# A hybrid decoder block: retention's projection as two Strassen passes, and retention itself beside the output projection

## The chip, the cores and the metric

The kernel runs on one core of a Trainium2 chip. The metric is device time in microseconds (us) of one execution of the whole program. The engines are TensorE (PE in the profile, with its weight loads shown apart as PEld), VectorE (DVE), ScalarE (ACT), GpSimd (POOL) and SyncE (SP, which issues most DMAs). PSUM has eight banks of 128x512 float32; they are what TensorE writes to.

## The reference

One decoder layer over 1024 tokens of width 1024, in float32:

```
h    = RMSNorm(x)
proj = h @ w_in                        # 1024 x 3584: rq rk rv rg (512 each), dq dk dv (512 each)
ret  = retention(rq, rk, rv)           # 8 heads of 64; rotary on q and k; chunks of 128 tokens
ret  = RMSNorm_per_head(ret) * silu(rg)
dif  = differential attention(dq, dk, dv)   # 4 heads, two causal softmax maps per head
x    = x + concat([ret, RMSNorm_per_head(dif)]) @ w_out
x    = x + (silu(h2 @ w_gate) * (h2 @ w_up)) @ w_down     # h2 = RMSNorm(x), d_ff = 2816
```

Retention of one head and one chunk of 128 tokens: `inner = (q k^T) * decay`, `o = inner v + (q * q_dec) state`, `state = state * chunk_dec + (k * k_dec)^T v`. The state makes the chunks of one head sequential.

## The kernel before

Every large product is done in three matmuls of the fast float32r type: an operand is split into a high half (a cast to float32r, on ACT) and a low half (the difference, on DVE), and `mm3` adds hi·hi, hi·lo and lo·hi. Small products (turns of tiles by the identity, retention's own matmuls, attention's values) are plain float32.

The program is a sequence of stages. In each stage the function `run(ops, main)` (line 509) takes eight steps of a main product, one for each 128 rows of the contraction, and puts small pieces of work between the steps. The tables `DIF_PLAN` (line 76) and `RET_PLAN` (line 104) say for each piece how many stages behind the product it runs, and behind which step. The order is pinned: instructions stay on their engine in the order in which they were issued. All pinned instructions pass through one helper (`issue`, line 375), so nearly all rows of the profile have line 376, and one goes by the names of tiles.

- Stages 0 to 31: projection and differential attention of 4 heads x 8 token tiles, `proj(g, t)` with 384 columns. The normed and turned activations stay on the chip as `hT` (tile name `act`). In `d_qz` GpSimd makes the cast `qz`; `rsqrt` is a power on GpSimd. The scores (`d_scores`, bank `big`) read `qz` two steps into the next stage.
- Stages 32 to 63: projection of retention, 4 pairs of heads x 8 token tiles, with 512 columns (q, k, v and gate of two heads): 24 matmuls of 128x512 a stage. Behind it go the pieces of the unit of two heads: `r_rot` (rotary, value scaling, gate), `r_turn`, `r_take` (ACT copies q and k out of PSUM, and q again by halves), `r_inner`, `r_mask`, `r_state`, `r_decay`, `r_out`, `r_sq` and `r_norm`. The inner products and the outputs have banks of their own, two of each (`it`, `o`).
- Three stages `o_proj(t, 0)` with the last pieces of retention, then `mid()`: the other 13 half-row tiles of the output projection, the norm, and the first 14 Strassen products of gate and up. The table `MID_PLAN` (line 121), some 200 rows written out by hand, places the small work there.
- Gate and up, 11 groups of 256 columns, each in seven products (Strassen's scheme over 2x2 blocks), and then down, in seven products of 11 chunks. Their order follows from program order and rings of tiles.

The weights of the projections are loaded one stage ahead (256 KB for each 128 rows) and split by ACT and DVE.

## Time and profile before

| | us |
| --- | --- |
| runs (three) | 1210.06, 1210.2, 1211.38 (median 1210.2) |
| span of the profiled execution | 1208.6 |
| differential stages | 0 to 250.9 |
| retention stages | 250.9 to 475.2 |
| output projection and norm | 475.2 to 587.3 |
| gate and up | 587.3 to 992.2 |
| down | 992.2 to 1208.6 |

The borders are read from the timeline (first and last matmul of the bank concerned). The page gives busy time for each engine, then the span in 40 slices, the DMA queues, the chain of work that ended last, and the costliest groups of instructions. A group's row has its busy time and the mean of one instruction behind the bar, and behind the next bar the idle time of the engine just before these instructions with what ended it. In a timeline a row starts with its start and its length, and the idle time before it stands in brackets. A run of equal instructions shares one row. Starts of TensorE's rows are firmer than their ends: matmuls overlap, so the distance of two starts is the time that one takes.

### The profile page before, as it was taken

The page shows a single profiled execution, that of the slowest core. Times are in us where ns is not written, and L with a number is a line of the kernel's source. Part 1 is how long each engine was busy: PE and PEld are TensorE (multiplying, and loading weights), DVE is VectorE, ACT ScalarE, POOL GpSimd, SP SyncE. Part 2 cuts the span into 40 slices and gives each one's busy share as a digit, 9 for nine tenths or more (in the row PEclk, how much of TensorE's full clock was granted, in tenths as well). Part 3 has the DMA queues.
Part 4 walks back from the last instruction along what each step waited for, and adds up shares of the span by engine and source line. Part 5 has one row for each costly group of instructions (what it writes and reads, how often), then busy time and mean ns, then how long its engine had stood idle before and what let it go on. Part 6 is the DMA issues. An engine that isn't in the chain of part 4 may idle for free.

```text
span 1208.6 us, 17360 instructions
## 1 busy us (share of the span) xinstructions
PE 1199.0 (99%) x5968; PEld 1020.0 (84%) x5968; DVE 834.1 (69%) x1501; ACT 537.6 (44%) x1194; POOL 556.6 (46%) x709
## 2 busy tenths in 40 slices
PE   8999999999999999999999999999999999999998
PEld 7898989888888888888888888888888888888887
DVE  6988888854444445545988765766657559698697
ACT  6866666653222233434634344333443434444442
POOL 2655555644444443200066556554566536254053
PEclk9999999999999999999999999999999999999999
DMA  7200011103111110332233323423333178943332
GB/s 209 62 28 27 28 30 35 45 10 97 48 40 36 40 40 27 122 123 79 61 123 118 109 96 114 131 83 92 105 113 127 65 238 287 366 129 96 96 122 79
DMA packets 97239, 117.08 MB, mean 97 GB/s; under 512 B 8960, under 2 KB 60288, under 8 KB 97152
## 3 DMA queue, kind: packets, MB, share of 16 engines
q1 hardware_dynamic: 95824, 115.38, 29.8%
q8 instruction: 47, 0.77, 0.3%
q10 hardware_dynamic: 1328, 0.60, 0.2%
q14 instruction: 40, 0.33, 0.1%
HBM read 87.38 MB, written 28.57 MB: 96 GB/s over the span
## 4 chain that ended last, share of the span: by engine, by line
PE 96%; DVE 2%; ACT 1%; DMA 0%; issue 0%; SPq 0%; ACTq 0%; DVEq 0%
PE pp L376 44%; PE h L376 27%; PE m L376 19%; PE big L376 3%; PE o L376 2%; PE it L376 1%; DVE act L376 0%; DMA more<-in_w_in_dram 0%; DVE q L376 0%; DVE acc L376 0%; ACT kh L376 0%; DVE wlo L376 0%; DVE kl L376 0%; DVE sum L376 0%; DVE kh L376 0%
## 5 line engine op out<-in xcount | busy, mean ns | idle before, releaser
L376 PE MATMUL pp<-whi,act 128*128 128x384 f32 (+1 forms) x896 | 286.4, 372 | 0.3 <-ACT whi L376 0.3
L376 POOL TENSOR_TENSOR sum<-rawp 128x512 f32<-128x512 f32 x100 | 142.1, 1423 | 174.2 <-DVE wlo L376 172.6
L376 ACT CAST whi<-sum 128x512 fp32r<-128x512 f32 x165 | 102.6, 622 | 202.2 <-POOL sum L376 66.0
L376 DVE TENSOR_TENSOR wlo<-sum,whi 128x512 fp32r<-128x512 f32 x165 | 165.7, 1005 | 35.2 <-ACT whi L376 35.0
L376 PE MATMUL h<-act,whi 128*128 128x512 f32 x608 | 187.2, 389 | 0.0
L376 PEld LDWEIGHTS pp<-whi,act 128*128 128x128 f32 x896 | 166.6, 188 | 15.1 <-ACT whi L376 0.7
L376 PE MATMUL pp<-wlo,act 128*128 128x384 f32 (+1 forms) x448 | 161.2, 360 | 0.6 <-DVE wlo L376 0.6
L376 POOL TENSOR_TENSOR sum<-wide 128x512 f32<-128x512 f32 x55 | 87.1, 1586 | 127.2 <-DVE wlo L376 100.2
L376 PEld LDWEIGHTS h<-act,whi 128*128 128x128 f32 x608 | 114.0, 188 | 23.6
L376 PE MATMUL pp<-wrh,act 128*128 128x512 f32 x384 | 131.3, 402 | 0.0
L376 PE MATMUL h<-act,wlo 128*128 128x512 f32 x304 | 118.3, 389 | 0.0
L376 DVE TENSOR_TENSOR wlo<-wide,whi 128x512 fp32r<-128x512 f32 x99 | 78.8, 819 | 32.6 <-ACT whi L376 32.6
L376 PE MATMUL pp<-act,whi 128*128 128x512 f32 (+2 forms) x320 | 97.2, 385 | 0.2 <-DVE act L376 0.2
L376 PE MATMUL m<-act,whi 128*128 128x512 f32 (+2 forms) x320 | 97.0, 385 | 0.0
L376 ACT CAST whi<-wide 128x512 fp32r<-128x512 f32 x99 | 59.3, 621 | 83.2 <-PE m L376 43.3
L376 PEld LDWEIGHTS pp<-wlo,act 128*128 128x128 f32 x448 | 84.6, 189 | 7.8 <-DVE wlo L376 1.2
L376 PEld LDWEIGHTS pp<-wrh,act 128*128 128x128 f32 x384 | 72.2, 188 | 14.3
L376 POOL TENSOR_TENSOR fsum<-c 128x512 f32<-128x512 f32 x55 | 79.4, 1454 | 9.6 <-DMA ffd<-fsum 9.6
L376 DVE TENSOR_TENSOR c<-c,h 128x512 f32<-128x512 f32 x86 | 56.8, 681 | 30.4 <-PE h L376 30.4
L376 PE MATMUL pp<-wrl,act 128*128 128x512 f32 x192 | 74.9, 390 | 0.0
L376 DVE TENSOR_TENSOR wlo<-rawp,whi 128x512 fp32r<-128x512 f32 x44 | 47.5, 1079 | 38.9 <-ACT whi L376 38.1
L376 PEld LDWEIGHTS pp<-act,whi 128*128 128x128 f32 x320 | 59.9, 188 | 12.2 <-DVE act L376 0.4
(163 smaller groups left out, 2514.2 us busy)
## 6 DMA issues: line engine op xcount, KB each, us to landing
wide<-ffd SPq DMA_DIRECT2D x77, 256.0 KB, 2.7
ffd<-fsum SPq DMA_DIRECT2D x55, 256.0 KB, 2.0
rawp<-in_w_gate_dram SPq DMA_DIRECT2D x22, 512.0 KB, 3.8
rawp<-in_w_up_dram SPq DMA_DIRECT2D x22, 512.0 KB, 3.8
wide<-in_w_down_dram SPq DMA_DIRECT2D x44, 256.0 KB, 5.4
raw<-in_w_in_dram SPq DMA_DIRECT2D x32, 256.0 KB, 2.8
ffd<-c SPq DMA_DIRECT2D x22, 256.0 KB, 2.0
raw<-in_w_in_dram SPq DMA_DIRECT2D x26, 192.0 KB, 2.5
```

The source lines that it names most:

```text
L376: i = getattr(self.engine, op)(*args, **kw)
```

## The change

Retention's projection is no longer 32 stages of 24 matmuls. Its 1024 x 1024 by 1024 x 2048 product is cut into two passes of 1024 columns (the q, k, v and gate columns of four heads each), and each pass is done by seven products of blocks half as long in every direction, as in Strassen's scheme. A product is four tiles (128 tokens) of four row blocks of `mm3`: 48 matmuls of 128x512. Pass `p=0` computes P1, P2, P4, P6, P7, P5, P3; pass `p=1` P1, P2, P6, P5, P3, P7, P4.

The sums of activation blocks that four of the products need are built in DRAM while the differential stages run: in stages 8 to 30 `s_sum` stores or copies a block (SP) or adds one to it with an accumulating DMA that GpSimd issues, two calls a stage, 40 accumulations in 20 stages. Later `x_sum` loads a sum and splits it. Sums of weight blocks are made per product out of two to four raw pages (`prepare`: GpSimd subtracts, ACT scales, DVE adds and splits). The products are combined by DVE (or ACT, or GpSimd once) into output tiles, which are stored in DRAM (`cd`) and read again by retention.

In the last three stages of the differential part, where the tail of attention still runs, `lead` does the first 72 matmuls of pass 0, and a table `LEAD` makes the weights of P4 there. From there to the first products of gate and up all work is a list of jobs with engine, duration and the keys that it reads and writes. `Plan` simulates the engines with these durations, four rounds, takes on each engine the ready job that is due first, and the jobs are issued, pinned, in the order of their starts. `RET_PLAN`, `MID_PLAN` and their pieces are gone.

Retention is done in units of four heads and 128 tokens (`unit`), 16 instead of 32. Four of them stand beside pass 1, twelve beside the output projection, whose tiles go in the order `PAIRS`. The unit has one bank each for its turn, its inner products, and its output with its state update. The differential part is otherwise as it was, and so are gate, up and down after their first products.

The first place is GpSimd in one differential stage. In the rows, `rs4` is the reciprocal root of q and k's mean squares, `qz` the cast, `mo` and `ro` the output's norm, `rowa` the attention's output. Before:

```order
L376 TENSOR_TENSOR rs4_1934<-ms4_1932,cs_77 128x4
L376 CAST qz1_186<-q_1995 64x128 x2
L376 TENSOR_SCALAR epso_2015<-ls_1975 128x1
L376 TENSOR_SCALAR mo_2023<-so_2021,epso_1902 128x1
L376 TENSOR_TENSOR ro_2025<-mo_2023,cs_77 128x1
L376 TENSOR_SCALAR rowa_94<-ob_2018,ro_2025 128x128
```

The same place in the change:

```order
L136 TENSOR_TENSOR rs4_2077<-ms4_2075,cs_77 128x4
L136 DMA sumd_196<-act_88 128x512 x2
L136 CAST qz0_185<-q_2144 64x128 x2
L136 TENSOR_SCALAR epso_2164<-ls_2120 128x1
L136 TENSOR_SCALAR mo_2172<-so_2170,epso_2045 128x1
L136 TENSOR_TENSOR ro_2174<-mo_2172,cs_77 128x1
L136 TENSOR_SCALAR rowa_95<-ob_2167,ro_2174 128x128
```

Two accumulating DMAs now stand between the root and the cast on GpSimd's queue.

The second place is TensorE in retention. Before, in a retention stage (`it` the inner products, `o` the output, `m` a state update or a turn, `pp` the projection):

```order
L376 MATMUL it_5280<-qbd1_3632,qkT_5253 128x256
L376 MATMUL m_5282<-vh_5194,qkr_5198 128x128
L376 MATMUL pp_5257<-whi_4493,act_87 128x512
L376 MATMUL pp_5257<-wlo_4494,act_87 128x512
L376 MATMUL pp_5257<-whi_4493,act_87 128x512
...
L376 MATMUL o_5302<-rg1_3628,qkT_5253 128x128
L376 MATMUL o_5302<-vh_5194,iT_5288 128x64 x2
L376 MATMUL m_5306<-cs_77,qkr_5269 128x128 x2
L376 MATMUL pp_5257<-whi_4709,act_87 128x512
```

In the change, ahead of the output projection's tile (4, 0) (`m_4011` is the turn's bank, `h_4014` the inner products' bank, `h_4015` the bank of output and state, `pp_3703` and `m_4010` turns of the mix for the output projection):

```order
L136 MATMUL h_4015<-wy_4669 128x64 x2
L136 MATMUL pp_3703<-cs_77,pr_3692 128x128 x4
L136 MATMUL h_4014<-wx_4668,wy_4669 128x256 x2
L136 MATMUL m_4010<-cs_77,rowa_94 128x128 x4
L136 MATMUL m_4011<-cs_77,wx_4668 128x128 x4
L136 MATMUL h_4015<-wy_4669,wx_4668 128x128 x2
L136 MATMUL h_4014<-wx_4668,wy_4669 128x256 x2
L136 MATMUL h_4015<-wy_4669 128x128
...
L136 MATMUL pp_3703<-cs_77,pr_3695 128x128 x4
L136 MATMUL m_4011<-cs_77,wx_4668 128x128 x4
```

Where nine matmuls of the projection stood between the inner products and the output, here turn, inner products and output of two units follow each other with no main product between.

The third place is DVE in pass 0, at products P7, P5 and P3 (`wlo` a low half of weights, `sx` a low half of an activation sum, `pr` a combination of products out of PSUM). In the retention stages before, DVE had rotary, mask, norm and one weight half a stage:

```order
L136 SCALAR_TENSOR_TENSOR wlo_2945<-spare_3700,g1col_78,whi_2944 128x512
L136 TENSOR_TENSOR sx_4002<-raw_4016,sx_4002 128x512
L136 SCALAR_TENSOR_TENSOR pr_3695<-h_4012,pr_3695 128x512
L136 TENSOR_TENSOR pr_3691<-pr_3691,h_4012 128x512
L136 SCALAR_TENSOR_TENSOR wlo_3064<-rowa_93,g1col_78,whi_3063 128x512
L136 SCALAR_TENSOR_TENSOR pr_3696<-h_4013,pr_3696 128x512
L136 TENSOR_TENSOR pr_3692<-pr_3692,h_4013 128x512
L136 TENSOR_TENSOR sx_4002<-raw_4017,sx_4002 128x512
```

DVE works on 128x512 tiles without a break there, with the halves for the next product between the combinations of this one.

The core of the diff:

```diff
-    NG = NDH + NRH // 2
-    W = [[None] * KC for _ in range(NG + 2)]
+    W = [[None] * KC for _ in range(NDH + 1)]
+    TERMS = {0: ((1, 0), (1, 1)), 1: (0, (0, 0)), 2: ((0, 0), (1, 0)), 3: (1, (0, 1))}
+    def s_sum():
+        n = 0
+        while summing and n < 1:
+            i, j, src, more_ = summing.pop(0)
+            if more_:
+                G.dma_start(sumd[i, j], src, accum_op=ALU.add)
+                n += 1
+            else:
+                SY.dma_start(sumd[i, j], src)
+    def lead():
+        for j, half in ((0, 0), (1, 0), (0, 1), (1, 1), (2, 0), (3, 0)):
+            for k in range(4):
+                h = hT[0][half][:, j]
+                wh, wl = W[NDH][4 * half + k]
+                mm3(lead_bank[j % 2], h[:, 0, k, :], h[:, 1, k, :], wh, wl, k == 0, k == 3)
+                yield
...
-        ops = place(DIF_PLAN, names, s, ND) + place(RET_PLAN, names, s - ND, NR)
+        ops = place(DIF_PLAN, names, s, ND)
+        if 8 <= s < ND - 1:
+            ops += [(1, s_sum), (5, s_sum)]
+        ops += LEAD.get(s, [])
...
+        def once(self):
...
+            while count < len(self.jobs):
+                best = None
+                for e, queue in waiting.items():
+                    if not queue:
+                        continue
+                    t = max(free[e], min(j.ready for j in queue))
+                    j = min((j for j in queue if j.ready <= t), key=lambda j: (j.late, j.n))
+                    if best is None or t < best[0]:
+                        best = t, j
...
+    def prepare(p, name, k, n):
+        ga, gb = g1(k), g1(4 + k)
...
+        elif name == "P6":
+            (ka, a), (kb, b) = difference(p, k)
+            kc, c = rawload(p, 1, 1, k)
+            act_copy(b, a, [ka], [kb], ga)
+            stt(c, c, gb, b, ALU.mult, ALU.add, [kb, kc], [kc])
+            halves_(n, kc, c)
...
+    def product(p, name, j, b, base):
+        h = BLOCK[name][:, j]
+        for k in range(4):
+            wh, wl = slot[base + k]
+            def go(k=k, wh=wh, wl=wl):
+                mm3(bank[b], h[:, 0, k, :], h[:, 1, k, :], wh, wl, k == 0, k == 3)
...
+    def unit(p, t, due=None):
+        (cak, ca), (cbk, cb) = ca_r(), cb_r()
+        dma(ca, cd[p, t, 0], [f"cd{p}{t}0"], [cak])
+        dma(cb, cd[p, t, 1], [f"cd{p}{t}1"], [cbk])
...
+        add("PE", 0.45, turn_, [qk], [f"b{b}"])
+        tk, qkT = qkT_r()
+        act_copy(qkT, bank[b], [f"b{b}"], [tk])
...
+        add("PE", 0.87, inner, [tk, bk], ["b6"])
...
+        add("PE", 1.35 if t else 0.9, out_, [tk, ik, vk] + ([old[0]] if t else []), ["b7o"])
...
+    PAIRS = [(0, 0), (1, 0), (0, 1), (1, 1), (2, 0), (3, 0), (2, 1), (3, 1), (4, 0), (5, 0), (4, 1), (5, 1),
+             (6, 0), (7, 0), (6, 1), (7, 1)]
...
+    for job in plan.times(4):
+        order["pinned"] = True
+        job.fn()
```

More of the change, by code (lines that the diff above doesn't have):

```diff
@@ L1072, in block_kernel @@
-    eased = set()
-    def n_rs(t):
-        ss2 = sums[t]
-        G.tensor_tensor(out=ss2[:, 0:1], in0=ss2[:, 0:1], in1=ss2[:, 1:2], op=ALU.add)
-        rsqrt(ss2[:, 0:1], ss2[:, 0:1], 1)
-    def n_scale(t, q):
-        h2[t] = x2[t]
-        V.scalar_tensor_tensor(out=h2[t][q], in0=x2[t][q], scalar=sums[t][:, 0:1],
-                               in1=gtile[:, q * 512:(q + 1) * 512], op0=ALU.mult, op1=ALU.mult)
-    def n_turn(t, q):
-        turned[t, q] = turn(h2[t][q])
+    bank = lead_bank + [bankm([P, 512]) for _ in range(2)] + [bankh() for _ in range(4)]
@@ new lines, in open_act, with lazy @@
+    def open_act(name, dtype):
+        shape = [P, 4, 2, 4, P] if dtype == F32R else [P, 8 * 512]
+        late[name] = act.tile(shape, dtype, tag="act", name=name)
+    def lazy(name):
+        return Lazy(lambda: late[name])
+    spare = [(f"R{i}", page) for i, page in enumerate(spare[:8])]
+    prk = [(f"pr{i}", pr[i]) for i in range(9)]
+    rowk = [(f"ra{i}", mixd[i]) for i in range(NT)]
+    rawk = [(f"raw{i}", wp.tile([P, 512], F32, tag="raw", name="raw", bufs=NRAW)) for i in range(2)]
@@ L1089, in part @@
+    blk = [sxt[1], lazy("b1"), sxt[2], lazy("b3"), hT[1][1], sxt[0], lazy("wo")]
+    sums = [small[:, 32 + 2 * t:34 + 2 * t] for t in range(NT)]
     def part(b, p):
         return [blk[b][:, p, i].rearrange("p k e -> p (k e)") for i in range(2)]
-    def n_hi(t):
-        A.copy(part(t // 4, t % 4)[0], turned[t, t // 4])
-    def n_lo(t):
-        hi, lo = part(t // 4, t % 4)
-        V.tensor_tensor(out=lo, in0=turned[t, t // 4], in1=hi.bitcast(F32), op=ALU.subtract)
-    def n_back(t, q):
-        A.copy(h2[t][q], turned[t, q])
@@ L1113, in f_lo @@
-    def f_lo(b, p):
-        hi, lo = part(b, p)
-        V.tensor_tensor(out=lo, in0=turned.pop((b, p, 0)), in1=hi.bitcast(F32), op=ALU.subtract)
-    def mix_turn(q):
-        tp = turned["mix", q] = bankm([P, 4, P])
-        for j in range(4):
-            T.transpose(tp[:, j, :], (mixr, mixd)[q][NT - 1][:, j * P:(j + 1) * P], ident)
-    def mix_part(q):
-        return [mT[3][:, 1, i, 4 * q:4 * q + 4, :] for i in range(2)]
-    def mix_hi(q):
-        A.copy(mix_part(q)[0], turned["mix", q])
@@ new lines, in block_kernel @@
+    blk_after.update({2: [marks["o", 7, 0]], 5: [marks["o", 7, 0]], 6: [marks["o", 7, 1]]})
+    for b in (2, 5, 6):
+        for p in range(4):
+            f_sum(b, p)
+    for o, n, tiles in FIRSTS:
+        while weights and free_slots:
+            if weights[0] == (1, 0):
+                first_load(1, 0)
+                first_load(1, 1)
+            first_weights(*weights.pop(0), free_slots.pop(0))
+        first_product(o, n, tiles)
+        if tiles.stop == 4:
+            free_slots.append(first_slot[o, n])
@@ L1175, in w_hi, with weights @@
-        def w_hi(self, n):
-            (i, j), other, *_ = PRODUCTS[n]
+            for j in range(2):
+                r = ap.tile([P, 4, 2, P], F32, tag="rawp", name="rawp", bufs=3)
+                SY.dma_start(r.rearrange("p k i e -> p k (i e)"),
+                             w[0, j * 512:(j + 1) * 512, f0 * P:(f0 + 2) * P].rearrange("(k p) e -> p k e", p=P))
+                self.raw.append(r)
+        def weights(self, n):
+            (i, j), other, op, *_ = PRODUCTS[n]
+            src = self.raw[j][:, :, i, :]
+            if other is not None:
+                both = wp.tile([P, 512], F32, tag="raw", name="sum", bufs=NRAW).rearrange("p (k e) -> p k e", e=P)
+                G.tensor_tensor(out=both, in0=src, in1=self.raw[other[1]][:, :, other[0], :], op=op)
+                src = both
```

1208 lines of the change are left out of this document (626 added, 582 removed).

## The prediction

> **What bounds the kernel now.** I read the page's busy line first, then the chain of waits, then a table of stretches cut at the stage borders, then the timeline inside single stages. The page of the kernel before:
>
> ```profile
> span 1208.6 us, 17360 instructions
> PE 1199.0 (99%) x5968; PEld 1020.0 (84%) x5968; DVE 834.1 (69%) x1501; ACT 537.6 (44%) x1194; POOL 556.6 (46%) x709
> PEclk9999999999999999999999999999999999999999
> PE 96%; DVE 2%; ACT 1%; DMA 0%; issue 0%; SPq 0%; ACTq 0%; DVEq 0%
> ```
>
> TensorE is busy 99% of the span, at a granted clock of 0.9 or more in every slice, and the chain that ends last is 96% TensorE. So work taken from TensorE is time won, unless the new order makes TensorE wait. The two stretches that the change rebuilds, in the table of stretches (length, then busy time and count of PE, PEld, DVE, ACT, POOL, then clock, DMA share, GB/s):
>
> ```profile
> 250.90:475.20 224.30, 224.30 (x1177) 190.68 (x1176) 103.67 (x288) 73.69 (x209) 98.78 (x182) 1.00 0.15 44
> 475.20:587.30 112.10, 111.89 (x565) 94.36 (x564) 64.64 (x106) 47.82 (x101) 15.14 (x35) 1.00 0.33 106
> ```
>
> Retention with its projection (224.3 us) has no idle TensorE at all, the output projection loses 0.2 us, and DVE fills 46% and 58%. There is nothing to win there but matmuls, and much to lose in waits.
>
> **What is removed.** The projection was 32 stages of 24 matmuls, 128x512 each; now it is 14 products of 4 tiles, 4 row blocks and 3 matmuls, so 672 instead of 768. The price of one is in the chain (start, length) and the price of a matmul behind a float32 piece in the TensorE timeline:
>
> ```profile
> 601.09 5.44 PE m L376 x24
> 361.35 0.47 PE L376 MATMUL pp<-whi,act 128*128 128x512 f32 x1
> 361.66 0.39 PE L376 MATMUL pp<-wlo,act 128*128 128x512 f32 x1
> 361.89 0.63 PE L376 MATMUL pp<-whi,act 128*128 128x512 f32 x2
> ```
>
> 24 in 5.44 us is 0.2267 us each, so 96 of them are 21.8 us. The first 512-wide matmul after a float32 piece is followed at 0.31 us (361.35 to 361.66), the next at 0.23 (361.66 to 361.89): some 0.083 us per piece. In the order of the change TensorE has 142 such pieces where it had 183, because units of four heads put twice the small matmuls side by side: 41 x 0.083 = 3.4 us. The small matmuls themselves stay (762 float32 rows in both orders). Floor: 1208.6 - 21.8 - 3.4 = 1183.4 us of span.
>
> **Part (a), the sums in the differential stages.** 40 accumulating transfers are issued by POOL, two back to back in each of 20 stages, between the reciprocal root rs and the cast qz. POOL in one stage (start, length, idle before), and the groups that price a row of POOL:
>
> ```profile
> 156.34 1.04 POOL L376 TENSOR_TENSOR rs<-ms,cs 128x4 f32<-128x4 f32 x1
> 159.04 0.64 POOL L376 CAST qz<-q 64x128 fp32r<-64x128 f32 x2 [1.66 <-ACT q L376]
> 160.59 0.27 POOL L376 TENSOR_SCALAR mo<-so,epso 128x1 f32<-128x1 f32 x1 [0.54 <-ACT sqo L376]
> L376 POOL CAST qz<-q 64x128 fp32r<-64x128 f32 x64 | 22.1, 346 | 58.3 <-ACT q L376 55.6 <-PE m L376 0.8
> L376 POOL TENSOR_SCALAR epso<-ls 128x1 f32<-128x1 f32 x32 | 8.8, 274 | 7.5 <-ACT p L376 4.1
> L376 POOL TENSOR_TENSOR sum<-wide 128x512 f32<-128x512 f32 x55 | 87.1, 1586 | 127.2 <-DVE wlo L376 100.2 <-DMA wide<-in_w_down_dram 27.0
> ffd<-c SPq DMA_DIRECT2D x22, 256.0 KB, 2.0
> ```
>
> The cover is POOL's idle time ahead of qz, 58.3/32 = 1.82 us a stage, and the 0.54 us before mo, 2.36 in all. What waits behind the two issues is qz, and behind it the scores on TensorE; then mo, ro, and the next stage's rs, on which the turn of q and k hangs. The trace of before has no DMA issued by POOL. Its price lies between the smallest and the largest row of POOL, 0.27 and 1.59 us: no stall up to 1.18 us each, and at 1.59 (2 x 1.59 - 2.36) x 20 = 16.4 us. A gain is excluded, since nothing is taken from POOL here. An issue touches no 128x512 operand and is nearest to the small row, so nearly nothing; but the first accumulation of each of the three groups also waits for its page's store (2.0 us for 256 KB) with qz behind it. I take 1, bounds 0 and 16.4. SP's 16 more stores and copies, and eight spills of mixd, cost nothing: no engine waits on them within many stages.
>
> **Part (b), the two passes.** TensorE has 600 x 0.2267 = 136 us of products after the lead, and 4 units of retention. By the table of stretches a two-head unit costs 224.3/32 - 5.44 = 1.57 us, so four heads 3.14: 148.6 us together. That has to cover DVE, whose rows here are priced by these groups:
>
> ```profile
> L376 DVE TENSOR_TENSOR wlo<-sum,whi 128x512 fp32r<-128x512 f32 x165 | 165.7, 1005 | 35.2 <-ACT whi L376 35.0
> L376 DVE TENSOR_TENSOR act<-sum,act 128x512 fp32r<-128x512 f32 x20 | 13.7, 686 | 1.8 <-ACT act L376 1.5
> L376 DVE SCALAR_TENSOR_TENSOR wlo<-raw,g1col,whi 128x512 fp32r<-128x512 f32 x16 | 11.9, 742 | 0.0
> L376 DVE TENSOR_TENSOR c<-c,h 128x512 f32<-128x512 f32 x86 | 56.8, 681 | 30.4 <-PE h L376 30.4
> L376 POOL TENSOR_TENSOR sum<-rawp 128x512 f32<-128x512 f32 x100 | 142.1, 1423 | 174.2 <-DVE wlo L376 172.6
> ```
>
> Over both passes DVE has about 101 rows with two SBUF operands and 54 with a PSUM one, and some 7 us of small ones: 101 x 0.742 + 54 x 0.681 + 7 = 119 us, 80% of TensorE's time. The tight place is pass one. Products P6, P7 and P5 need 12, 12 and 8 SBUF rows and 4, 4 and 8 PSUM rows while TensorE works 3 x 48 x 0.2267 = 32.6 us: 34.6 us of DVE at 0.742 and 43.1 at 1.005. P4 ahead of them gives TensorE 10.9 us and DVE only four rows, and the weights sit in two alternating sets, so the work for P6 can run there: 37.6 to 47.1 us of DVE against 43.5. Bounds: 0, and 43.1 - 32.6 = 10.5 if nothing runs ahead. At 1.005 with the work ahead it is 3.6. I take 2, the middle of 0 and 3.6, because POOL's 12 rows of 1.42 us in P6, P7 and P5 cover only half of that time.
>
> On the difference between 1005 and 686 ns the Trainium skill (SBUF — State Buffer, "Who interferes with whom") says that a DVE instruction with two SBUF inputs contends with a GpSimd instruction that reads SBUF. The trace agrees as far as these groups go, since the slow group runs among POOL's sums. By that rule only overlapping rows slow down, and term (b) would be 0; by the mean of 1.005 on every row it would be 3.6.
>
> Loads are the other supply: about 104 pages of w_in, 16 sums, 32 stores, 8 reads and 8 pages of w_out, 256 KB each, 44 MB in 165 us, 267 GB/s. Two answers of the DMA view bound that:
>
> ```profile
> DMA packets 8173, 10.12 MB, mean 101 GB/s; under 512 B 448, under 2 KB 6080, under 8 KB 8166
> q1 hardware_dynamic: 8166, 10.04, 31.3%
> DMA packets 10668, 19.46 MB, mean 324 GB/s; under 512 B 1187, under 2 KB 1187, under 8 KB 10664
> q1 hardware_dynamic: 10664, 19.41, 92.7%
> wide<-in_w_down_dram SPq DMA_DIRECT2D x22, 256.0 KB, 5.4
> 1000.00:1060.00 60.00, 60.00 (x267) 49.67 (x266) 50.84 (x62) 24.83 (x43) 25.63 (x16) 1.00 0.93 324
> ```
>
> The first two rows (700 to 800 us) have mostly 1 KB packets, as the new w_in pages do; the last four (1000 to 1060) show 324 GB/s with TensorE idle for nothing, only the landing grows to 5.4 us. 267 lies under that, so loads add nothing to the 2.
>
> **Part (c), retention beside the output projection.** Twelve units lie among 384 main matmuls and 32 groups of four turns. The unit's chain, from the timeline of one two-head unit, with the ACT copies' groups:
>
> ```profile
> 363.50 0.38 PE L376 MATMUL o<-rg,qkT 128*128 128x128 f32 x2
> 364.37 0.28 ACT L376 ACTIVATE sqr<-o 128x128 f32<-128x128 f32 x1 [3.41 <-PE o L376]
> 364.68 0.28 DVE L376 TENSOR_REDUCE ss<-sqr 128x2 f32<-128x128 f32 x1 [1.75 <-ACT sqr L376]
> 365.05 0.64 POOL L376 TENSOR_TENSOR ss<-ss,eps 128x2 f32<-128x2 f32 x1 [1.51 <-DVE ss L376]
> 365.76 0.72 POOL L376 TENSOR_TENSOR rs<-ss,cs 128x2 f32<-128x2 f32 x1
> L376 DVE TENSOR_TENSOR on<-o,rs 128x128 f32<-128x128 f32 x32 | 8.9, 280 | 0.0
> L376 ACT COPY qkT<-m 128x256 f32<-128x256 f32 x32 | 11.8, 368 | 0.0
> L376 ACT COPY aT<-m 128x512 f32<-128x512 f32 x20 | 11.7, 587 | 36.1 <-PE m L376 36.1
> ```
>
> From the output matmul (363.50) to the end of on (365.76 + 0.72 + 0.28) the output bank is held 3.3 us, and there is one such bank now instead of two. TensorE's time per unit is (384 x 0.2267 + 12 x 3.14)/12 = 10.4 us without the turns, so where main matmuls lie between the units the bank is free again. But TensorE's order has about eight units with no main matmul inside them: turn, inner and output follow each other, and TensorE then waits for the ACT copies (0.59 + 2 x 0.37 = 1.33 us) and the mask (0.68). With hand-offs of about 0.1 us (364.28 to 364.37) and small matmuls of neighbouring units between, that is 0 to some 2.5 us each; and four pairs of the output projection wait up to 0.59 + 0.68 = 1.3 us for the halves of the turned mix. Bounds 0 and 8 x 2.5 + 4 x 1.3 = 25. I take 9: half the chain, 1.1 us, at each of the eight, since two units mostly stand beside each other there.
>
> **Sum.** 1183.4 + 1 + 2 + 9 = 1195.4 us of span. The median of the runs, 1210.2, is 1.6 above the profiled span, which gives a forecast of **1197.0 us**.
>
> **Rivals.**
>
> R1, every wait is hidden: 1183.4 + 1.6 = 1185.0. For it: before, TensorE lost 0.2 us in 336 with its orders written out in tables. Against it: the eight bare units.
>
> R2, DVE sets the pace of P6, P7 and P5: (b) is 10.5 instead of 2, 1205.5. For it: 1005 ns is the mean of 165 rows. Against it: POOL reads there only half the time and P4 leaves room.
>
> R3, the single banks and the ACT copies set the pace of the bare units: (c) is 25 instead of 9, 1213.0, level with before or a little slower. For it: each unit's step needs three engines, and POOL's 1.42 us rows stand ahead of its small ones. Against it: 10.4 us of TensorE per unit.
>
> R4, the other side: POOL's issues in the differential stages cost more than their cover. One mechanism: qz and the next rs come late, and the scores and the turn of q and k, which have no slack, wait for them. Without (a) the time is 1196.0; it passes 1212.6 when each stage loses 0.83 us, so from (0.83 + 2.36)/2 = 1.6 us an issue, just over POOL's largest row; at 2.0 us it is 1196 + 20 x 1.64 = 1229. For it: no row prices such an issue, and the two are back to back. Against it: six times the small row is needed.
>
> A rule that speaks for R4: the Trainium skill (SBUF — State Buffer, "A bandwidth-pool intuition that's wrong") states that descriptors of a software-issued DMA are written by GpSimd, which waits while a DVE copy holds the shared port, 0.62 us alone and 3.1 overlapped; DVE's kh copies are in each of these stages. By 0.62 term (a) is 0; by 3.1 it would be 77 us, an estimate from that page; no run here shows it yet.
>
> **How the numbers follow.** Forecast 0.52 (its own range 1189 to 1207), R1 0.13, R2 0.13, R3 0.10, R4 0.12. About 0.2% either way, 1207.8 to 1212.6, is what a measurement can't tell from no change. Faster: 0.52 + 0.13 + most of R2 (0.11) = 0.76. Slower: 0.10 of R4 and half of R3 = 0.15. The rest, 0.09, is same. The range 1187 to 1213 leaves out R4 (0.12) and part of R1 (0.08).
>
> **What would show it.** In the profile after: 96 fewer 512-wide matmuls and about 1174 us of TensorE busy time (1199.0 - 25.2); qz's idle time shrunk from 1.82 us but still waiting for ACT, with stages up to 250 us as long as before (right), or qz released by POOL's own DMA row and later products 20 us late (R4); TensorE idle behind DVE's halves of P6, P7 or P5 under 4 us in all (R2 if 10); idle behind ACT copies and the mask at the bare units near 9 us (R3 if 25). The forecast fails most easily in (a) and (c), whose prices no row of before shows.

## The result: slower, and the profile after

The changed kernel takes 1239.9 us (median, 1239.2 to 1242.9) against 1210.3 for the kernel before, a ratio of 1.0247 (95% interval 1.0232 to 1.0262). The forecast was 1197.0. (Of e12_ahead and e15_lead_dve, below, one of two runs was disturbed and is left out; their times are single runs.) The page of the change:

```profile
span 1240.8 us, 17596 instructions
PE 1196.0 (96%) x5872; PEld 1009.0 (81%) x5872; DVE 907.5 (73%) x1460; ACT 570.6 (46%) x1188; POOL 666.3 (54%) x728
PE 78%; DMA 6%; DVE 6%; POOL 4%; issue 3%; ACT 2%; SPq 0%; DVEq 0%; POOLq 0%; ACTq 0%
```

TensorE has the 96 instructions less that were forecast (5968 to 5872), but idles 45 us where it idled 10. The chain that ended last is TensorE for 78% of the span instead of 96%; 18% of it now runs through DMAs, DVE, GpSimd and ACT. The stretches of both kernels, cut at the same places of the work (end of the differential part; first product of gate; the point 168 matmuls of 128x512 later, from which both run level; end), the kernel before first:

```profile
0.00:243.90 243.90, 238.12 (x1467) 217.85 (x1468) 202.75 (x510) 158.82 (x438) 132.47 (x278) 1.00 0.20 57
243.90:573.70 329.80, 329.80 (x1699) 278.77 (x1699) 161.62 (x385) 117.47 (x305) 115.56 (x220) 1.00 0.19 61
573.70:620.00 46.30, 46.09 (x226) 39.34 (x225) 44.72 (x70) 24.37 (x45) 7.21 (x7) 1.00 0.23 69
```

```profile
0.00:246.80 246.80, 239.02 (x1466) 219.46 (x1467) 203.31 (x510) 158.84 (x438) 168.02 (x314) 0.99 0.57 119
246.80:592.10 345.30, 320.91 (x1588) 263.90 (x1587) 230.44 (x352) 144.89 (x289) 163.32 (x186) 0.98 0.59 192
592.10:652.10 60.00, 51.11 (x241) 41.56 (x240) 53.51 (x64) 31.42 (x59) 39.44 (x26) 0.94 0.22 70
652.10:1240.80 588.70, 584.97 (x2581) 484.05 (x2579) 420.24 (x536) 235.47 (x405) 295.46 (x204) 1.00 0.41 134
```

| stretch | before | after | difference | forecast |
| --- | --- | --- | --- | --- |
| differential part | 243.9 | 246.8 | +2.9 | +1 |
| retention and output projection | 329.8 | 345.3 | +15.5 | -25.2 + 2 + 9 = -14.2 |
| first products of gate and up | 46.3 | 60.0 | +13.7 | 0 |
| the rest | 588.6 | 588.7 | +0.1 | 0 |

So 45.4 us of span have to be explained: 1.9, 29.7 and 13.7. The middle stretch of the change, cut again: the lead (its first 72 products), the two passes, the output projection:

```profile
242.20:273.30 31.10, 28.36 (x154) 23.40 (x153) 20.69 (x39) 13.97 (x35) 19.35 (x25) 1.00 0.58 187
273.30:457.00 183.70, 165.97 (x761) 132.80 (x761) 135.57 (x192) 81.86 (x147) 83.91 (x79) 0.98 0.80 258
457.00:592.10 135.10, 131.18 (x699) 111.56 (x698) 78.54 (x134) 50.88 (x115) 63.27 (x89) 0.97 0.31 98
```

The passes move 258 GB/s with the DMA engines 80% busy, and TensorE is idle 17.7 us in them. What one such wait hangs on can be followed through the timelines of five engines:

```profile
384.00 0.96 SPq L136 DMA_DIRECT2D rawp<-in_w_gate_dram  x2
385.06 0.45 SPq L136 DMA_DIRECT2D rowa<-in_w_in_dram  x1
389.50 0.37 SPq L136 DMA_DIRECT2D rowa<-in_w_in_dram  x1
392.89 1.29 POOL L136 TENSOR_TENSOR rowa<-rowa 128x512 f32<-128x512 f32 x1 [5.64 <-DMA rowa<-in_w_in_dram]
394.43 1.29 POOL L136 TENSOR_TENSOR spare<-spare 128x512 f32<-128x512 f32 x1
395.75 0.75 DVE L136 SCALAR_TENSOR_TENSOR spare<-spare,g1col,rowa 128x512 f32<-128x512 f32 x1 [4.49 <-POOL spare L136]
397.90 1.28 POOL L136 TENSOR_TENSOR rowa<-rowa 128x512 f32<-128x512 f32 x1 [2.18 <-DMA rowa<-in_w_in_dram]
399.21 0.72 ACT L136 ACTIVATE rowa<-rowa,g1col 128x512 f32<-128x512 f32 x1 [3.86 <-POOL rowa L136]
400.47 0.69 DVE L136 TENSOR_TENSOR wlo<-pr,whi 128x512 fp32r<-128x512 f32 x1 [3.04 <-ACT whi L136]
401.55 0.82 PE L136 MATMUL h<-wy,wx 128*128 128x128 f32 x4 [3.11 <-DVE wx L136]
```

A page of w_in is issued at 385.06, right behind two loads of 512 KB for gate, and lands 7.8 us later; the plan counted on 2.6. GpSimd's difference waits 5.64 us for it, and DVE's sum of weights waits 4.49 us for GpSimd. The next page is issued at 389.50 and GpSimd waits for it until 397.90, 8.4 us after its issue. ACT's scaling of that page waits 3.86 us for GpSimd; behind the scaling, in ACT's frozen order, stands a cast, for which DVE's next half waits 3.04 us; and behind that half stands the norm of a retention unit (`wx`), for which TensorE then waits 3.11 us. The wait is booked on DVE and a retention tile; its root is two late loads.

### The profile page after: what moved, and what is told of

The parts are those of the page before. It is cut to its first block, busy times and chain, and to the rows that moved or that the text cites. A ratio compares the mean times of both kernels' runs of the same rounds, so it can differ in the third digit from the quotient of the medians.

```text
span 1240.8 us, 17596 instructions
## 1 busy us (share of the span) xinstructions
PE 1196.0 (96%) x5872; PEld 1009.0 (81%) x5872; DVE 907.5 (73%) x1460; ACT 570.6 (46%) x1188; POOL 666.3 (54%) x728
## 4 chain that ended last, share of the span: by engine, by line
PE 78%; DMA 6%; DVE 6%; POOL 4%; issue 3%; ACT 2%; SPq 0%; DVEq 0%; POOLq 0%; ACTq 0%
PE h L136 34%; PE pp L136 25%; PE m L136 17%; PE big L136 2%; DMA spare<-in_w_in_dram 2%; DVE wlo L136 1%; DMA raw<-sumd 1%; DMA rowa<-in_w_in_dram 1%; POOL sum L136 1%; POOL spare L136 1%; DVE pr L136 1%; POOL wx L136 0%; DMA sumd<-sumd 0%; ACT whi L136 0%; DVE sx L136 0%
## 5 line engine op out<-in xcount | busy, mean ns | idle before, releaser
L136 PE MATMUL pp<-whi,act 128*128 128x384 f32 (+1 forms) x624 | 191.7, 358 | 1.2 <-ACT whi L136 0.7
L136 PEld LDWEIGHTS pp<-whi,act 128*128 128x128 f32 x624 | 116.2, 189 | 6.2 <-ACT whi L136 0.9
L136 PE MATMUL h<-sx,whi 128*128 128x512 f32 x360 | 112.6, 394 | 7.4 <-ACT rowa L136 7.1
L136 PE MATMUL pp<-wlo,act 128*128 128x384 f32 (+1 forms) x312 | 108.6, 348 | 0.6 <-DVE wlo L136 0.6
L136 PEld LDWEIGHTS h<-sx,whi 128*128 128x128 f32 x360 | 67.4, 189 | 21.6 <-ACT rowa L136 7.6
L136 PE MATMUL h<-whi 128*128 128x512 f32 x196 | 76.5, 390 | 0.0
L136 PE MATMUL h<-whi,wlo 128*128 128x512 f32 x196 | 76.3, 389 | 0.0
L136 PE MATMUL h<-wlo,whi 128*128 128x512 f32 x196 | 76.2, 389 | 0.0
L136 PE MATMUL h<-sx,wlo 128*128 128x512 f32 x180 | 70.5, 392 | 0.4 <-DVE wlo L136 0.4
L136 PE MATMUL h<-b,whi 128*128 128x512 f32 x176 | 54.3, 390 | 0.0
```

Source lines behind the costliest of these rows:

```text
L136: i = getattr(self.engine, op)(*(now(a) for a in args), **{k: now(a) for k, a in kw.items()})
```

## The experiments

Each run has one edit, or several that are named, and is compared with the change's 1239.9 us where no other run is named. The stretches are read from the timelines at the same products as above (us; lead, passes, output projection, first products of gate).

| run | diff. part ends | lead | passes | out. proj. | gate | span | median |
| --- | --- | --- | --- | --- | --- | --- | --- |
| before | 243.9 | | | | 46.3 | 1208.6 | 1210.3 |
| change | 246.8 | 31.1 | 183.7 | 135.1 | 60.0 | 1240.8 | 1239.9 |
| e1_lag | 246.1 | 31.2 | 168.6 | 135.2 | 64.9 | 1230.0 | 1232.6 |
| e2_rows2k | 245.5 | 32.6 | 178.5 | 132.4 | 60.2 | 1233.2 | 1236.0 |
| e3_fsum | 246.7 | 31.2 | 182.8 | 134.2 | 56.1 | 1235.0 | 1236.2 |
| e4_sums_sp | 244.1 | 31.2 | 182.0 | 132.2 | 60.0 | 1233.4 | 1235.3 |
| e5_ffn_dve | 247.0 | 31.2 | 181.1 | 132.6 | 51.3 | 1227.2 | 1230.0 |
| e6_diff_dve | 247.1 | 32.2 | 176.6 | 136.8 | 63.5 | 1240.3 | 1239.9 |
| e7_half | 245.5 | 31.2 | 165.9 | 132.3 | 60.1 | 1219.0 | 1222.0 |
| e8_lag_ffn | 245.8 | 31.2 | 170.9 | 133.7 | 53.8 | 1219.5 | 1221.0 |
| e9_half_ffn | 246.2 | 32.5 | 166.2 | 132.4 | 51.3 | 1212.6 | 1215.3 |
| e10_lead | 245.5 | 28.0 | 181.4 | 134.0 | 60.1 | 1232.9 | 1234.0 |
| e11_lag65 | 245.3 | 31.2 | 175.3 | 133.9 | 54.4 | 1224.1 | 1226.8 |
| e12_ahead | 246.1 | 32.5 | 167.3 | 135.5 | 54.0 | 1219.5 | 1221.3 |
| e13_three | 247.5 | 28.0 | 164.0 | 132.3 | 51.3 | 1207.1 | 1208.4 |
| e14_actq | 245.3 | 31.2 | 171.0 | 133.8 | 54.3 | 1219.7 | 1220.7 |
| e15_lead_dve | 245.4 | 28.2 | 169.5 | 133.8 | 53.7 | 1214.5 | 1216.4 |
| e16_lag_passes | 245.8 | 28.0 | 175.6 | 135.2 | 51.5 | 1220.1 | 1224.2 |

Executions of one kernel lie up to some 3 us from their median here, and the profiled one of the change is 3.0 us above its own (1242.9 against 1239.9), so a difference of two spans is good to some 3 us. Five rows have the same order of TensorE from the passes to the end of the output projection, and their loads are untouched: the change, e3_fsum, e4_sums_sp, e5_ffn_dve and e10_lead. Their passes take 181.1 to 183.7 us and their output projections 132.2 to 135.1, so a stretch repeats to some 3 us too.

**Late loads: does the plan start them too late?** (e1_lag)

```diff
-        return add("SP", 0.06, lambda: SY.dma_start(to, src), r, w, lag=2.6, **kw)
+        return add("SP", 0.06, lambda: SY.dma_start(to, src), r, w, lag=5.2, **kw)
```

> The plan takes 2.6 us for every transfer; in the profile of the change loads of w_in pages land after 4.7 to 5.0 us and the sums after 5.1. Here the plan alone is told 5.2 us, all else as in the change. If the passes lose their time because loads are started too late for the order that was frozen (late loads), the two passes (273 to 457 us) shrink by 10 us or more: 1222 to 1231 us. If the transfers themselves are the limit (79% of the DMA engines' time there), or DVE is, an order that counts on later loads gains under 4 us: 1236 to 1244.

The passes fell by 13 to 15 us, to 168.6, with the same bytes landing hardly earlier (4.7 to 4.9 us instead of 5.0). The gate stretch grew by 4.9 (the order behind the passes was drawn up anew too; what in it costs this was not followed), so only 7.4 us are left in the time. For the question the stretch counts, not the total: an order that counted on the longer latency lost less to it.

**Are small packets the reason?** (e2_rows2k)

```diff
-        return rows[:, 2 * nu:2 * nu + 2, p * 256:(p + 1) * 256]
+        return rows[:, 2 * nu + p, :].rearrange("p (a b) -> p a b", b=256)
```

> The order of the change is kept, but each page of w_in is read as 128 rows of 2 KB in a piece instead of 256 rows of 1 KB (other columns, so the projection of retention is another matrix and the output is not the reference's). If the loads are late because they are many small packets, the landing falls from 5.0 towards 3 us and the passes shrink by 10 us or more, 1222 to 1231 us. If the landing is set by bytes or by what else is under way, it stays at 4.5 to 5 us and the time at 1236 to 1243.

The landing fell only from 5.0 to 4.7 us and the passes by 3 to 5, to 178.5. The number of packets is a small part.

**Are bytes?** (e7_half)

```diff
-        dma(page.rearrange("p (a b) -> p a b", b=256), win_block(p, nu, 4 * kap + k), (), [key])
+        dma(page.rearrange("p (a b) -> p a b", b=256)[:, 0:1], win_block(p, nu, 4 * kap + k)[:, 0:1], (), [key])
```

> The order of the change is kept, but each page of w_in in the passes is loaded by half (128 KB; the other half keeps what the page held, so retention's weights are others). If bytes under way set the landing, it falls from 5.0 to 3 us or less, and if late loads are what holds the passes, they shrink from 183.7 us by 15 or more: 1218 to 1226 us. If the landing falls and the passes keep their length, loads are not the cause: 1236 to 1242.

The DMA view of the passes, the change first (273.3 to 457), then this run (272.1 to 438), then this run's rows of the stretches (passes, output projection):

```profile
q1 hardware_dynamic: 37998, 47.26, 79.3%
spare<-in_w_in_dram SPq DMA_DIRECT2D x53, 256.0 KB, 5.0
raw<-sumd SPq DMA_DIRECT2D x16, 256.0 KB, 5.1
```

```profile
q1 hardware_dynamic: 26869, 35.87, 67.9%
spare<-in_w_in_dram SPq DMA_DIRECT2D x53, 128.0 KB, 3.1
raw<-sumd SPq DMA_DIRECT2D x16, 256.0 KB, 3.7
```

```profile
272.10:438.00 165.90, 159.92 (x762) 131.50 (x760) 135.51 (x192) 81.97 (x147) 80.98 (x79) 1.00 0.68 217
438.00:570.30 132.30, 128.51 (x699) 108.39 (x697) 79.37 (x134) 50.82 (x115) 63.99 (x90) 1.00 0.31 100
```

With the order of all engines unchanged, half the bytes of w_in bring the landing to 3.1 us and the passes down by 15 to 18 us, to 165.9; TensorE's idle time in them falls from 17.7 to 6.0 us. Sums, of which nothing was taken, land 1.4 us earlier too. DVE's busy time in the passes is the same (135.6 and 135.5 us), and so, nearly, are ACT's (81.9 and 82.0) and GpSimd's (83.9 and 81.0): it was not the engines' own work that held them for these 15 to 18 us. Late loads are shown as their cause. Up to 3.4 us of it are the clock, 0.98 in the change's passes and 1.00 here, which was halved after such waits (last section).

**Do they wait behind stores in SP's queue?** (e14_actq, on e8_lag_ffn below)

```diff
-        dma(cd[p, t, nu], page, [key], [f"cd{p}{t}{nu}"])
+        add("ACT", 0.06, lambda: A.dma_start(cd[p, t, nu], page), [key], [f"cd{p}{t}{nu}"], lag=5.2)
```

> As the run with 5.2 us for a transfer and DVE's sums (1221.0), but the 32 stores of the passes' results are issued on ACT's queue instead of SP's, where they wait for DVE's results ahead of loads. If loads are late because they stand behind such stores, 3 to 8 us come back: 1213 to 1218. If bytes under way set the landing, nothing does, 1220 to 1223, or ACT's own queue now waits and it is 1223 to 1230.

Nothing: 1220.7 against 1221.0, passes 171.0 against 170.9. The stores are not in the loads' way.

**The first products of gate: late weights, or GpSimd beside DVE?** (e3_fsum, then e5_ffn_dve, which has both edits)

```diff
-        eng, dur, e = ("POOL", 1.45, G) if b in (2, 5, 6) else ("DVE", 0.8, V)
+        eng, dur, e = "DVE", 0.8, V
...
-            eng, dur, e = ("POOL", 1.45, G) if o else ("DVE", 0.8, V)
+            eng, dur, e = "DVE", 0.8, V
```

> The twelve activation sums of gate and up for blocks 2, 5 and 6 are made by DVE (0.69 us a row in the profile of before) instead of GpSimd (1.68 us). From the first product of gate and up to the place where both orders run level the change lost 13.7 us, with one wait of 7.2 us. If that wait is GpSimd's row of sums and weight sums, 6 to 10 us come back: 1230 to 1234 us. If it is the late load of the gate weights or DVE's own queue, under 3 us: 1237 to 1243.

> All 512-wide sums around the first products of gate and up go to DVE: the activation sums of blocks 2, 5 and 6 as in the run before, and also the weight sums of up. In the change GpSimd is busy 39.4 of the 60.0 us there, and DVE's halves take up to 1.79 us where the kernel before, with GpSimd busy 7.2 of 46.3 us, has 0.69. If DVE is slowed by GpSimd's rows (contention), the stretch falls from 60.0 to 47 to 50 us, 1227 to 1231 us in all, with DVE's rows back at 0.69. If the late load of gate's weights is the cause (a wait of 7.2 us of TensorE ends with it), the stretch stays above 54 us and the time above 1233.

The first edit alone gave 3.7 us of the time (3.9 of the stretch), less than expected; both gave 9.9 (8.7 of the stretch, 60.0 to 51.3, where 47 to 50 were expected). Groups of DVE in that stretch, before, in the change, and with both edits, and the last run's row of the stretch:

```profile
L376 DVE TENSOR_TENSOR act<-sum,act 128x512 fp32r<-128x512 f32 x14 | 9.6, 684 | 0.0
```

```profile
L136 DVE TENSOR_TENSOR sx<-sum,sx 128x512 fp32r<-128x512 f32 x8 | 11.4, 1428 | 2.1 <-ACT sx L136 1.8
L136 DVE TENSOR_TENSOR wlo<-raw,whi 128x512 fp32r<-128x512 f32 x8 | 8.1, 1018 | 0.0
L136 DVE TENSOR_TENSOR pr<-pr,h 128x512 f32<-128x512 f32 x4 | 2.7, 679 | 0.1
```

```profile
L136 DVE TENSOR_TENSOR wlo<-raw,whi 128x512 fp32r<-128x512 f32 x8 | 5.4, 688 | 0.1
L136 DVE TENSOR_TENSOR sx<-sum,sx 128x512 fp32r<-128x512 f32 x8 | 5.2, 689 | 0.0
```

```profile
587.20:638.50 51.30, 48.56 (x241) 40.68 (x241) 49.41 (x78) 28.33 (x52) 7.85 (x7) 1.00 0.24 76
```

A half made of two SBUF operands takes 1.43 us where GpSimd is busy 39.4 of 60.0 us, and 0.69 where it is busy 7.9 of 51.3; rows with one operand in PSUM (`pr<-pr,h`) take 0.68 either way. Inside the change's stretch it can be seen row by row: the 14 additions and subtractions of DVE on two SBUF tiles that have no 512-wide row of GpSimd beside them take 0.68 to 0.69 us, the 28 that have one take 0.68 to 1.80, 1.22 in the mean. DVE now does 78 rows in less busy time (49.4 us) than 64 before the edit (53.5). (Of five other halves, `wlo<-rawp,whi`, two still take 1.77 us in the last run, with one of GpSimd's remaining sums beside them.)

TensorE's longest wait in the stretch, 7.2 us, vanished too, but it does not hang on DVE's slow rows alone. SP's longest wait for GpSimd from 590 to 632 us (total, times, longest), and ACT just before TensorE goes on:

```profile
SPq L136 <- POOL raw L136: 23.6, 2, 16.0
626.25 0.62 ACT L136 CAST whi<-sum 128x512 fp32r<-128x512 f32 x1 [2.86 <-POOL sum L136]
```

A load of gate's weights waits 16.0 us for the buffer that a sum of GpSimd still has to read, in a queue of GpSimd's rows of about 1.66 us each; GpSimd's next sum waits for that load, ACT's cast for that sum, and behind the cast stands the copy that frees TensorE's bank. Both edits together take away DVE's slowed rows and GpSimd's own slow queue; how the 8.7 us divide between the two is not shown.

**The same in the passes?** (e6_diff_dve)

```diff
-        tt(a, a, b, ALU.subtract, [ka, kb], [ka], "POOL", 1.45)
+        tt(a, a, b, ALU.subtract, [ka, kb], [ka])
...
-            tt(d, d, c, ALU.subtract, [kd, kc], [kd], "POOL", 1.45)
+            tt(d, d, c, ALU.subtract, [kd, kc], [kd])
```

> The differences of weight pages in the two passes (28 rows) are made by DVE instead of GpSimd. If GpSimd's rows slow DVE's there (means of 0.99 to 1.13 us for halves with two operands in SBUF), DVE does this work in the time that it gains, and the passes shrink by 4 us or more: under 1236. If late loads set the passes, nothing changes within 3 us; if DVE's own work does, they grow: 1241 to 1248.

The passes shrank by 5 to 7 us, to 176.6, but the lead, the output projection and gate grew by 1.1, 1.7 and 3.5 and the time stayed at 1239.9. The order is another from the passes on, so the time does not tell how much of the passes is contention. DVE's rows tell a part: it does 26 rows more there (218 instead of 192) in only 4.5 us more (140.1 us instead of 135.6), where 26 rows at 0.69 us would be 17.9. So some 13 us of DVE's time in the passes had gone to rows that were slow beside GpSimd's; how much of that TensorE waited for is not shown.

**The accumulating transfers.** (e4_sums_sp)

```diff
-                G.dma_start(sumd[i, j], src, accum_op=ALU.add)
+                SY.dma_start(sumd[i, j], src)
```

> The 40 accumulating transfers that GpSimd issues become plain stores of the same bytes issued by SP (so the additions of activation blocks in DRAM are left out, and the products that use them are of other numbers). The differential stages took 2.9 us longer in the change. If GpSimd's issues (1.08 us each) make that, the last matmul of these stages comes back by 2 to 3 us, 1236.5 to 1238.5 us in all; if the traffic does, nothing changes, 1239 to 1241. By the rival of the prediction that these issues are the main loss it would be 1215 or less.

The differential part came back by 2.7 of its 2.9 us, and the time by 4.6, more than expected; the other 2 us lie in the passes and behind them (182.0 and 132.2) and are within what runs differ by. The rows of the change that price an issue, from the view of the tile of the sums (shortest, median and longest ns) and from the groups, the cast behind the issues:

```profile
L136 POOL DMA_DIRECT2D sumd<-act x40: 948/1148/1213, 70.1 to 212.7; - x40
```

```profile
L136 POOL CAST qz<-q 64x128 fp32r<-64x128 f32 x64 | 23.9, 373 | 19.7 <-ACT q L136 16.7 <-PE m L136 0.8
```

An issue takes 1.15 us of GpSimd (median), the idle time ahead of qz fell from 58.3 to 19.7 us, and it did not run out. So where do the 2.9 us lie? The starts of the stages say: 1.1 us at the very beginning, before the first accumulation (70.1 us), and 1.7 in a single stage. The change's first stretch, that stage in the kernel before and in the change, and what happens in it:

```profile
0.00:15.20 15.20, 12.44 (x45) 9.20 (x46) 7.12 (x13) 9.09 (x16) 1.41 (x9) 0.89 0.97 281
159.20:166.10 6.90, 6.77 (x42) 5.94 (x41) 5.64 (x16) 4.51 (x15) 4.17 (x9) 1.00 0.11 31
160.40:169.00 8.60, 6.99 (x40) 5.94 (x40) 5.96 (x16) 4.49 (x15) 7.69 (x13) 1.00 0.64 114
160.67 1.87 POOL L136 DMA_DIRECT2D sumd<-act  x2 [2.08 <-DMA sumd<-sumd]
166.99 0.42 DVE L136 TENSOR_TENSOR qkn<-pp,rs 128x256 f32<-128x256 f32 x1 [2.12 <-POOL rs L136]
167.56 0.41 PE L136 MATMUL m<-cs,qkn 128*128 128x128 f32 x2 [1.24 <-DVE qkn L136]
```

The beginning took 14.1 us before, 14.2 in e4_sums_sp and 13.8 in e7_half, where nothing is edited there; the change's clock was 0.89 in it, and this 1.1 us is not the accumulations'. In the stage from 160.4, GpSimd's accumulation waits 2.08 us for the copy of a sum in DRAM; GpSimd is late by that with all that follows, DVE waits for the next `rs` and TensorE for the turn of q and k. In e4_sums_sp this stage takes 6.9 us again. In the other 19 stages with accumulations the starts keep their distance to the kernel before within 0.1 us: there the issues cost nothing.

**The lead.** (e10_lead; then e15_lead_dve on e8_lag_ffn)

```diff
+    LEAD = {s: [op for op in ops if op[1] not in (t4_minus, t4_scale, t4_sum)] for s, ops in LEAD.items()}
...
-        G.tensor_tensor(out=a, in0=a, in1=b, op=ALU.subtract)
+        V.tensor_tensor(out=a, in0=a, in1=b, op=ALU.subtract)
```

> In the last three differential stages the preparation of P4's weights (GpSimd's differences, ACT's scaling, DVE's sums) is left out, so P4 takes raw pages as weights; the loads stay. There the 72 leading matmuls take 31.2 us (242.2 to 273.3); with 24 of them and the same tail of attention a stage of the kernel before took 28.8 for 72, with pieces of retention in it. If that preparation holds up the tail, the 31.2 fall to 27 to 29 us and the time by 2 to 4: 1236 to 1238. If the copies of the two lead banks or the tail itself set it, the 31.2 stay: 1239 to 1241.

> As the run with 5.2 us for a transfer and DVE's sums (1221.0), but the eight differences of weight pages in the lead are made by DVE (0.69 us) instead of GpSimd (1.4 us). If GpSimd's rows there hold up the tail of attention (its norm is on GpSimd, and DVE's rows slow down beside it), the 72 leading matmuls take 28 to 29.5 us instead of 31.2 and the time is 1217 to 1219.5. If the work as such does, on whichever engine, 1220.5 to 1223.

Without the preparation of P4 the lead takes 28.0 us instead of 31.1, as expected, and the time is 1234.0, 2 us below what was expected of it. With all of it, but its eight differences on DVE, 28.2: it was GpSimd's eight rows in the queue of the attention tail, not the work.

**Do the causes add, and what is left?** (e8_lag_ffn: e1 and e5; e9_half_ffn: e7 and e5; e13_three: e5, e10 and an eighth of each page)

> Two edits together: the plan told 5.2 us for a transfer (which alone gave 1232.6) and the sums around gate and up on DVE. If the two losses are separate places, the gains add: 1218 to 1224 us, with the stretch from the first product of gate under 52 us. If the second only moved what the first won, 1229 to 1233.

> Half of each w_in page in the passes (as before: retention's weights are others) together with the sums around gate and up on DVE. Alone they gave 17.9 and 9.9 us. If late loads and contention at gate and up are two separate causes, the sum is 1240 - 27 to 29 = 1210 to 1213 us, near the kernel before but not under it, which leaves some 13 us to 1197 for other causes. If they overlap, 1216 to 1222.

> Three causes away at once, in the order of the change: only an eighth of each w_in page is loaded in the passes, the preparation of P4 in the lead is left out (retention's weights are others by both), and the sums around gate and up are on DVE. If these three are what the prediction missed, the time is within 5 us of the forecast, 1196 to 1203 us, and the passes fall from 166 to 158 to 161 us (136 us of products and seven units of 3.14). If waits inside retention's units hold the rest, the passes stay at 164 us or more and the time at 1206 to 1212.

They add, roughly: 7.4 + 9.9 = 17.3 gave 18.9 (the gate stretch, 53.8, was not under 52), and 17.9 + 9.9 = 27.8 gave 24.6, which with 1215.3 us lies between the two ranges. The third expectation failed and its rival's numbers came: with all three causes away the time is 1208.4, ratio 0.998 to the kernel before (0.9966 to 0.9989), 11 us over the forecast. Its stretches (lead, passes, output projection, gate) and TensorE's two longest waits (total, times, longest):

```profile
242.80:270.80 28.00, 27.45 (x155) 23.47 (x154) 16.86 (x37) 11.42 (x31) 8.66 (x17) 1.00 0.62 200
270.80:434.80 164.00, 158.82 (x761) 131.90 (x760) 133.26 (x191) 82.68 (x148) 81.24 (x79) 1.00 0.56 168
434.80:567.10 132.30, 128.49 (x700) 108.49 (x699) 80.15 (x135) 50.84 (x116) 63.56 (x89) 1.00 0.32 99
567.10:618.40 51.30, 48.55 (x241) 40.67 (x240) 49.38 (x78) 28.25 (x52) 7.88 (x7) 1.00 0.25 77
```

```profile
PE h L136 <- ACT wx L136: 3.7, 4, 1.6
PE h L136 <- DVE wy L136: 2.3, 3, 0.9
```

From the end of the differential part (247.5) to the first product of gate (567.1) it needs 319.6 us, 10.2 less than the kernel before, where 14.2 were forecast. The rest to the forecast is 2.6 us in the differential part, 5.0 in gate's first products and 4.0 here. These 4.0 are not waits: TensorE idles 9.5 of the 319.6 us, where 2 + 9 were forecast, most of it inside retention's units (behind ACT's and DVE's copies). Its busy time, 310.1 us, is what exceeds the forecast (329.8 - 25.2 = 304.6).

**Tuning the plan further.** (e11_lag65, e12_ahead, e16_lag_passes)

```diff
-        return add("SP", 0.06, lambda: SY.dma_start(to, src), r, w, lag=5.2, **kw)
+        return add("SP", 0.06, lambda: SY.dma_start(to, src), r, w, lag=6.5, **kw)
...
-    GAP, GAP_PE, AHEAD = 0.15, 0.6, 4.0
+    GAP, GAP_PE, AHEAD = 0.15, 0.6, 8.0
...
-        return add("SP", 0.06, lambda: SY.dma_start(to, src), r, w, lag=5.2, **kw)
+        return add("SP", 0.06, lambda: SY.dma_start(to, src), r, w, lag=2.6 if "o" in marks else 5.2, **kw)
```

> As the run with 5.2 us for a transfer and DVE's sums (1221.0), but the plan is told 6.5 us, above the median landing of 4.7 to 5.3 and below the longest on the chain of waits (7.8). If what is left in the passes (170.9 us, where half the bytes gave 165.9) is loads that come later than planned, 2 to 5 us more come back: 1216 to 1219. If the transfers' bytes set it, 1220 to 1225.

> As the run with 5.2 us and DVE's sums (1221.0), but every operand is due 8 us ahead of its product instead of 4. If products wait because operands are finished at the last moment, 2 to 5 us come back: 1216 to 1219. If pages and transfers limit how early the work can be done, nothing changes: 1219 to 1224.

> All mends that keep the computation: DVE makes the differences in the lead and all sums around gate and up, and the plan is told 5.2 us for transfers of the two passes and 2.6 us, as in the change, for those behind them (they land after 2.4 to 3.4 us there). If the order behind the passes was worse only because it counted on slow transfers, 2 to 4 us come back from 1216.4: 1212 to 1215, still not under the kernel before. If not, 1215.5 to 1218.

6.5 us was worse than 5.2 (1226.8 against 1221.0, outside both ranges), due times did nothing to the time (passes 3.6 us shorter, lead and output projection 3.1 longer), and the last, on e15_lead_dve, lost 8 us (1224.2, outside both ranges too) where a gain was expected: its passes, planned with the same 5.2 us as in e15_lead_dve, took 175.6 instead of 169.5. A new number reorders everything, and that alone was worth some 6 us of the passes here. The best kernel with the change's own computation is e15_lead_dve, 1216.4 us: it wins back 23 us of 30 and does not beat the kernel before.

## Why the prediction was wrong

**The work removed: the matmuls right, the busy time not.** TensorE issues 96 instructions less. Its busy time was to fall to 1174 us and was 1196.0, and 1182.7 with the three causes away. In the middle stretch it fell by 19.7 of the forecast 25.2 us in e13_three; which price is off (the 3.4 us for float32 pieces, or the work of units and turns) was not measured apart.

**(a), about right, for a reason that the sum had named and left out.** I took 1 us; one stage lost 1.7, and the other 1.1 us of the 2.9 are not the accumulations'. The bound was sound: an issue lies between 0.27 and 1.59 us, at 1.15, just under the 1.18 up to which no stage stalls, and nineteen stages do not stall. The loss is the wait of an accumulation for the page under it, with qz and the next rs behind it: the prediction says that such a wait exists, and then that SP's copies cost nothing since no engine waits on them. GpSimd waited 2.08 us on one. This is R4's mechanism, in one stage and not in twenty: 1.15 is not 1.6, and R4 fell. The sentence on the Trainium skill (SBUF — State Buffer, "A bandwidth-pool intuition that's wrong"), 3.1 us beside DVE's copies, is not borne out for the issues: the longest of 40 took 1.21 us, and the 18 with a DVE cast of kh beside them took no longer (median 1.10) than the 22 without (1.20). The page's figure is the time of a whole transfer; these 40 land 3.9 to 7.0 us after their issue.

**(b), the step that failed most.** "Loads add nothing to the 2." I compared the rate needed (267 GB/s; 258 were measured) with the highest rate seen, and said in the same sentence that the landing there grows to 5.4 us. In down TensorE was busy 60.00 of 60 us in spite of that; here `Plan` had drawn up an order in which each load arrives 2.6 us after its issue, the loads landed after 5.0, and in a frozen order every late arrival holds up whatever stands behind the instruction that waits for it. Price: 15 to 18 us in the passes by e7_half. R2, DVE's own pace, did not decide: DVE was busy 135.6 us in the passes, where 119 were counted, but in e13_three it is hardly less (133.3 us) and the passes take 164.0. (The passes also hold seven units instead of four, by the order that `Plan` chose: 136 + 7 x 3.14 = 158 us without waits.)

**(c), the number near, the waits under half.** Nine us were taken for waits in the output projection and its mix. Its stretch holds 384 matmuls, nine units (36 inner matmuls at four a unit; the plan had put three of the twelve ahead, beside the last product) and 23 groups of four turns beside the units' own:

```profile
L136 PE MATMUL h<-wx,wy 128*128 128x256 f32 x36 | 9.7, 393 | 1.1 <-ACT wx L136 1.1
```

Four turns take 0.35 us in the passes and 0.08 goes to the matmul behind them, so 384 x 0.2267 + 9 x 3.14 + 23 x 0.43 = 125.2 us, an estimate, and the stretch took 135.1 in the change and 132.3 in e7_half: 9.9 and 7.1 more. But TensorE idles only 3.9 and 3.8 us of that, 1.1 of it behind ACT's copies `wx`. The bare units cost less than half of what was taken, R3 (25) did not come, and the rest is TensorE's own work above these prices, in the change also a stretch at half clock (last section). That the sum comes near 9 is luck in part.

**What was not in the sum.** The first products of gate and up stand in no term. Seventeen of their activation and weight sums had gone from DVE to GpSimd, and that was put at nothing without a reason. It cost 8.7 us of the 13.7 there by e5_ffn_dve; the other 5.0 stay open. The rule I had weighed for the passes (the Trainium skill, SBUF — State Buffer, "Who interferes with whom": a DVE instruction with two SBUF inputs contends with a GpSimd instruction that reads SBUF) names one part of it, and the trace agrees: 1.43 us against 0.69, and no change for rows with an operand in PSUM. The other part is that GpSimd takes 1.66 us for a sum that takes DVE 0.69, and that loads and ACT wait in turn for GpSimd's queue. The lead was put at nothing too: 3.1 us, by GpSimd's eight rows in front of the attention tail's own.

Together: 0.7 in (a), 1.1 at the beginning, 15 to 18 in the passes, 3.1 in the lead, 8.7 at gate, some 29 to 32 of the 45.4 us. Some 5.0 at gate and the rest in the middle (the clock, TensorE's work above its price) were not taken apart. Of the 45.4 us, some 3 are no more than the distance of the profiled execution from the median.

## What to carry to other kernels

A static order is only as good as its latencies under load: price a transfer by its landing in the busiest stretch of the trace that moves as many bytes, not by a quiet one, and ask what stands behind the instruction that waits for it. Work handed from DVE to GpSimd is not free even when both have room: here a sum took 1.66 us on GpSimd and 0.69 on DVE, and DVE's own rows on two SBUF operands took about twice as long beside it, so the handing over lost more than it saved. Cut even a small loss by stages before you price it: all that the accumulations cost lay in one stage of twenty, and was not the price of an issue. And read the code behind the changed region as closely as the region itself: nearly a third of this loss was in a stretch whose arithmetic had not changed.
